# Slot sizes of four SBUF pools rounded to multiples of 256 bytes in a hybrid decoder layer

## The chip, the cores and the metric

The kernel runs on one core of a Trainium2 chip, in one launch. The metric is the device time of the whole program in microseconds (us), as a median of several runs. The profiled execution is one run taken with the hardware profiler; its span reaches from the first to the last instruction.

## The reference

One decoder layer over 2048 tokens of 1024 features, all in float32. Cut to what matters:

```python
h = rmsnorm(x, mix_norm_w)
proj = h @ w_in
y = concatenate([s5_mixer(proj[:, :c_u], ...), ssd_mixer(proj[:, c_u:], ...)])
x = x + y @ w_out                                   # output projection
h = rmsnorm(x, xa_norm_w)
x = x + cross_attention(h, rmsnorm(mem, ...), wq, wk, wv, wo)   # 4 heads, 256 memory tokens
h = rmsnorm(x, ffn_norm_w)
gv = h @ w_up                                       # 1024 -> 2 x 2816
g = causal_dwconv(gv[:, :D_FF], conv_w, conv_b)     # width 3
x = x + (silu(g) * gv[:, D_FF:]) @ w_down           # 2816 -> 1024
return rmsnorm(x, final_norm_w)
```

## The kernel before

**Products.** TensorE multiplies a stationary operand (128 x 128, loaded first) by a moving one (128 x 512). Each float32 operand is split into a high and a low half of 12 significant bits (`halves`, L95: the copy to the high half on ScalarE at L98, the difference to the low half on VectorE at L99). A float32 product is then three matmuls (`mm3`, L123 to L125: high by high, high by low, low by high). So each 512-column float32 product costs one L98, one L99 and a third of the work of the three lines on TensorE. `products` (L999) computes a 2 x 2 block product by seven products instead of eight, in the order `ORDER = (1, 6, 5, 3, 7, 4, 2)`; each of the seven is called m here, and is 12 matmuls long.

**Stages.** They follow one another and share SBUF: when one is over its pools are closed, and the next opens its own over the same bytes.
- Mixer and memory: first norm, input projection, both mixers, keys and values. Not touched. Its pools have names with k, a and s5 in front.
- `stage_b` (L1085): output projection with residual (stationary: halves of y in pool A; moving: W_out in the rings Q0 to Q3), then scores and values of the cross-attention by `products` over eight pairs of token tiles each (stationary: halves of the left factors in A; moving: the right factors in Q0 to Q6). The ring `qp` hands out eight tiles of Q0, then of Q1 and so on, so each m has one Q pool of its own. The first m of each `products`, m = 1, has Q4; m = 6, the second, has Q5; m = 5, the third, Q6; and the last, m = 2, has Q3.
- `stage_up` (L1305): two blocks of 1024 tokens by 22 feature tiles, one `products` each. Stationary: halves of the weights, from the ring `wp`: two tiles at a time from pools V, V, W, W, W, W, W, W, W in turn, a pair (high and low half) for each product, so that of nine products in a row two have V and seven have W. Moving: the right factors in H1 to H7, one pool for each m. Raw weights and factors land in pool R by SyncE's queue (L111) ahead of the split.
- `stage_down` (L1410): seven products m = 0 to 6, each over the eight pairs of token tiles and 11 tiles of features, 33 matmuls for one pair. Stationary: halves of the activations in pools B and C in turn; moving: halves of the weights in the ring W0, W1, W2, W3, W4, eight tiles at a time, 22 tiles for one product. Raw activations land in A, raw weights in R.

**Pools.** `Kit.pools` (L55) lays a stage's pools one behind the other in the order of the call, and all three stages start at the same byte. A slot is as long as the tile (n float32 values per partition), so the lengths are 2048 bytes for n = 512 and 4096 for n = 1024, except for four pools: M in `stage_b` (4 slots of 568 values, of which L1092 uses 512), G and C in `stage_up` (4 slots of 568 values, 520 used; one slot of 992), and O in `stage_down` (2 slots of 1136, 1024 used). `reuse_waits="tile"` makes a new tile wait for the last use of those older tiles that lie on its own bytes. Each engine and each queue takes its instructions in order, so an instruction that waits holds up all that stand behind it on its engine.

Of the kernel before, what the change touches and what calls it, by code (L numbers as in the profile page):

```python
# [9 lines left out]
F32 = mybir.dt.float32  # L10
F32R = mybir.dt.float32r
# [4 lines left out]
P = 128  # L16
# [8 lines left out]
def bcol(a, n):  # L25
    """[p, m] as [p, m, n], each value repeated n times"""
    return a.rearrange("p (a b) -> p a b", b=1).to_broadcast([a.shape[0], a.shape[1], n])


class Kit:  # L30
    """the pools that every stage shares, and the steps that all of them use"""
# [23 lines left out]
    def pools(self, cx, pre, *specs):  # L55
        """pools in this order in memory; each tile waits only for those on its own bytes. A function per pool that takes a tile"""
        def one(nm, bufs, n=512):
            p = cx.enter_context(self.tc.tile_pool(name=pre + nm, bufs=bufs, reuse_waits="tile"))
            return lambda dt=F32: p.tile([P, n], dt, tag=nm, name=nm)
        return [one(*s) for s in specs]  # L60

    def gain(self, i, kt):
        """a norm's weights over feature tile kt, one per partition"""
        return self.gains[:, i * 8 + kt:i * 8 + kt + 1]
# [30 lines left out]
    def halves(self, src, hi, lo, scale=None):  # L95
        """hi + lo = src (times scale), both of 12 significant bits"""
        if scale is None:
            self.S.activation(hi, src, AF.Copy)  # L98
            self.V.tensor_tensor(lo, src, hi.bitcast(F32), op=ALU.subtract)  # L99
        else:  # L100
            self.S.activation(hi, src, AF.Copy, scale=scale)
            self.V.scalar_tensor_tensor(lo, src, scale, hi.bitcast(F32), op0=ALU.mult, op1=ALU.subtract)  # L102
# [24 lines left out]
    def rstd(self, out, ss, scale, eps):  # L127
        """(ss * scale + eps) ** -0.5"""
        n = out.shape[1]
        self.V.tensor_scalar(out, ss, scale, eps, op0=ALU.mult, op1=ALU.add)  # L130
        self.G.tensor_tensor(out, out, self.m05[:, 0:1].to_broadcast([P, n]), op=ALU.pow)  # L131

    def norm(self, x, xs, w=None):
        """xs = x / rms(x) over rows of 1024, times w"""
        ss = self.sm.tile([P, 1], F32, tag="ss", name="ss")
        self.S.activation(xs, x, AF.Square, accum_out=ss)
        self.rstd(ss, ss, 1.0 / 1024, 1e-6)
        if w is None:
            self.V.tensor_scalar(xs, x, ss[:, 0:1], None, op0=ALU.mult)
        else:  # L140
            self.V.scalar_tensor_tensor(xs, x, ss[:, 0:1], w, op0=ALU.mult, op1=ALU.mult)

    def tr4(self, src, hf):
        """four 128-column blocks of src, transposed"""
        p = self.ps()
        for q in range(4):
            c = (hf * 4 + q) * 128
            self.TE.transpose(p[:, q * 128:q * 128 + 128], src[:, c:c + 128], self.ident)
        return p

    def exp(self, pool, x, n, tag):
        """exp to float32's accuracy, for small tiles"""
        V = self.V
# [20 lines left out]
class MixerIn:  # L174
    """first norm, input projection, conv, SSD; blocks of 512 tokens"""

    def __init__(self, k, cx, a, dram, T):
# [40 lines left out]
        self.tri = c([P, P], "tri")                       # 1 where column >= row  # L218
# [8 lines left out]
        self.last = c([P, P], "last")                     # 1 in the last row  # L227
# [12 lines left out]
        self.wd = c([P, 8, 24], "wd", F32R)               # per feature tile, the high parts, then the low ones  # L240
# [24 lines left out]
    def norm1_direct(self):  # L265
        """block 0 straight into its two halves"""
# [51 lines left out]
    def conv(self, p, j):  # L318
        """silu of the causal conv of width 4; the taps are halved, so c * (1 + tanh(c)) is the silu"""
# [14 lines left out]
    def zgate(self, p, i):  # L334
        """2 silu(z)"""
        k = self.k
        th = k.t()
        k.S.activation(th, p, AF.Tanh, scale=0.5)
        z = self.zp.tile([P, 512], F32, tag=f"z{i}", name="z")
        k.V.scalar_tensor_tensor(z, th, 1.0, p, op0=ALU.add, op1=ALU.mult)  # L340
        return z

    def dtprep(self, hs, b):
        k, V, S, TE = self.k, self.k.V, self.k.S, self.k.TE
        p = k.ps()
        for q, (h, l) in enumerate(hs):                    # both parts of the weights with the high ones of h, then high with low
# [14 lines left out]
        s, s2, q = sm("s"), sm("s2"), sm("q")             # log(1 + e) = 2 atanh(e / (2 + e))  # L361
# [38 lines left out]
    def ssd(self, b, pr, dd, xs, Bs, Cs, zs, sqacc):  # L400
        """the six heads of two groups, four chunks of 128 tokens"""
# [3 lines left out]
        L = self.lp.tile([P, 4, 6, P], F32, tag="L", name="L")      # [s, c, h, l] = exp(a_cs[l] - a_cs[s]), 0 for l < s  # L405
# [150 lines left out]
def s5_setup(k, a, d, up, NJ):  # L556
    """the S5 group's step over 8 tokens: input maps, output maps, Toeplitz part, decay and rotations"""
# [22 lines left out]
    # sin and cos, reduced by pi / 2  # L580
# [31 lines left out]
    # powers 0..8 of the transition, [p, g, power]  # L612
# [20 lines left out]
    for s in range(8):                                    # the same, falling  # L633
# [3 lines left out]
    # (transition - 1) / lambda  # L637
# [27 lines left out]
    def comb(gs, A, X, B, Y, op):  # L665
        """[p, 4 g, 8 powers, 16 c] = A * X op B * Y"""
# [95 lines left out]
def stage_s5(k, a, d, T):  # L762
    """S5 group over the whole sequence, as a generator"""
# [132 lines left out]
class Memory:  # L896
    """G = wq k^T and VW = v wo per head, from the normed memory"""
# [4 lines left out]
    def prep(self):  # L902
        k, nc = self.k, self.k.nc
        # features on partitions: [f, (kt pair: kt, m)]
# [15 lines left out]
    def proj(self, name, then, n=1):  # L920
        """(mem w)^T, [d, (d tile pair: d tile, m)]"""
# [21 lines left out]
    def pairs(self, name, at, then):  # L943
        """the split rows of the four heads, one head ahead from piece `at` of the one before"""
# [54 lines left out]
def products(k, terms, tmp, put, after):  # L999
    """The four blocks of a product of 2 x 2 blocks by seven products (Winograd's form), with the left factors  # L1000
    a11, s2 = s1 - a11, s1 = a21 + a22, s4 = a12 - s2, s3 = a11 - a21, a22, a12 (in ORDER) and the right ones
    b11, t2 = b22 - t1, t1 = b12 - b11, b22, t3 = b22 - b12, t4 = t2 - b21, b21.
    put(i, j, x, y, op) takes block (i, j), which is x op y; y (for (1, 0): x) may be written over, but not for (1, 1)"""
# [28 lines left out]
def squares(k, x, junk):  # L1032
    """sum of squares of a row, given as its halves"""
# [14 lines left out]
def h3(k, d, p, x0, x1, tmp):  # L1048
    """right factors of the FFN's first product from the normed rows of a pair of tiles"""
# [29 lines left out]
def ring(n, pools):  # L1079
    """tiles from several pools in turn, n at a time"""  # L1080
# [4 lines left out]
def stage_b(k, cx, a, d, T, after):  # L1085
    """output projection with its residual, cross-attention with its residual, third norm"""
# [5 lines left out]
    xl, xp, q4, mp, ap, *qs, fp = k.pools(cx, "b", ("L", 2, 1024), ("X", 6, 1024), Q(4), ("M", 4, 568), ("A", 16), Q(0), Q(1), Q(2), Q(3), Q(5), Q(6), ("F", 10))  # L1092
# [9 lines left out]
    W, ys = {}, {}  # L1102

    def yprep(t, cuts):
        """halves of y's row of tiles, the columns between cuts at a time"""
# [20 lines left out]
    def factors(nm, j):  # L1126
        """t1, t2, t3, t4 of a right side"""
# [36 lines left out]
    def xprep(p):  # L1164
        xs = []
        for t in (2 * p, 2 * p + 1):
# [4 lines left out]
            k.rstd(rq[t], ss, 256.0 / 1024, 256.0 * 1e-6)      # 1 / (16 rms)  # L1171
# [133 lines left out]
def stage_up(k, cx, a, d, T, NF=22):  # L1305
    """the FFN's two branches, its conv and gate; blocks of 1024 tokens.
    [gate; value] = W^T h by seven products of half-size blocks instead of eight (Winograd's form): over the two branches,
    the two halves of the features and the even and odd tiles of the tokens"""
# [3 lines left out]
    wa, ev, up, h1, gp, wb, cp, *hs, rp, sp = k.pools(cx, "u", ("V", 4), ("E", 8), ("U", 4), H(1), ("G", 4, 568), ("W", 14), ("C", 1, 992), H(3), H(7), H(4), H(2), H(6), H(5),  # L1312
# [15 lines left out]
    def weights(i):  # L1328
        """the seven left factors, one at a time"""
# [27 lines left out]
    def rest():  # L1357
        """third norm of the last pairs of tiles"""
# [51 lines left out]
def stage_down(k, cx, a, d, out, T, NK=11):  # L1410
    """the FFN's output projection with its residual, last norm.
    Seven products instead of eight, one after the other over all pairs of token tiles"""
# [4 lines left out]
    xa, w0, xb, rp, ar, sp, cb, fp, *ws, wr, ca = k.pools(cx, "d", ("X", NT // 2, 1024), W(0), ("Y", NT // 2, 1024), ("O", 2, 1136), ("A", 6), ("S", 2), ("C", 6), ("F", 1, 1024),  # L1417
                                                          W(3), W(4), W(1), W(2), ("R", 4), ("B", 6))
    wp, ac = ring(8, [w0] + ws[2:] + ws[:2]), ring(6, [ca, cb])
    # left: (tile of the pair, half of ff), right: (half of ff, half of d), targets: (tile, half of d, sign)  # L1420
# [125 lines left out]
def layout(inp):  # L1546
    """the inputs as the chip wants them: reshapes, transposes and copies only"""
# [36 lines left out]
```

## Time and profile before

| | us |
|---|---|
| median of 3 runs | 2743.06 (2741.9 to 2744.83) |
| profiled execution, span | 2742.6 |
| ScalarE busy in it | 1322.4 |
| VectorE busy in it | 2119.5 |
| GpSimd busy in it | 484.5 |

The span lies 0.5 us below the median of the runs, and the page tells nothing of what lies around it. In the views, PE is TensorE's matmul, PEld its loading of the stationary operand, DVE is VectorE, ACT ScalarE, POOL GpSimd and SPq SyncE's queue of DMAs. Matmuls overlap one another in the pipe, so a matmul that "takes" 0.39 us can be followed by the next after 0.23 us: the rate is read from start to start. A row of the timeline gives start, duration, engine, line, operation, output and inputs (ps<-H,W: the moving operand lies in one of the H pools and the stationary one in W), count, and in brackets idle time before it with what ended it. Buffer and pool numbers are left out of the names: Q stands for Q0 to Q6, W of `stage_down` for W0 to W4.

### The profile page before, as it was taken

What the parts mean: (1) busy time and instruction counts of PE and PEld (TensorE: products, weight loads), DVE (VectorE), ACT (ScalarE), POOL (GpSimd) and SP (SyncE); (2) the same over time, 40 slices, a digit from 0 to 9 for tenths busy, and PEclk for the clock granted to TensorE, in tenths of its full rate; (3) what the DMA queues carried; (4) which work ended last, traced back from release to release, by engine and by line L of the source; (5) the groups of instructions that cost most, each with busy time, mean ns of one, the idle gap of its engine ahead of it and who ended that gap; (6) DMA issues with size and microseconds to landing.
All of it is one profiled execution on the core that took longest, in us unless ns stands there. A gap on an engine that the chain in (4) does not pass through costs nothing. (4 is left out here: it accounts for less than half of the span.)

```text
span 2742.6 us, 38944 instructions
## 1 busy us (share of the span) xinstructions
PE 2680.1 (98%) x12744; PEld 2201.9 (80%) x12744; DVE 2119.5 (77%) x4032; ACT 1322.4 (48%) x2661; POOL 484.5 (18%) x991
## 2 busy tenths in 40 slices
PE   8999999999899999999999999999999999999997
PEld 6878878787798888887878888888888887788876
DVE  8688887887786646778779778889878777677776
ACT  5565455544445314788635445345434334433333
POOL 0000000159812210201301223111111110000000
PEclk9999999999999999999999999999999999999999
DMA  5453243432377954537753334435222227887886
GB/s 194 139 162 127 90 134 107 122 98 85 110 262 240 334 197 181 183 136 251 249 185 122 119 115 132 126 89 177 86 79 85 77 62 263 276 296 225 261 264 203
DMA packets 238851, 455.57 MB, mean 166 GB/s; under 512 B 29432, under 2 KB 71416, under 8 KB 238648
## 3 DMA queue, kind: packets, MB, share of 16 engines
q1 hardware_dynamic: 182312, 341.38, 37.8%
q0 software_dynamic: 27728, 92.82, 10.5%
q10 hardware_dynamic: 28608, 18.88, 2.2%
q8 instruction: 101, 1.65, 0.3%
q14 instruction: 102, 0.84, 0.1%
HBM read 338.09 MB, written 114.29 MB: 165 GB/s over the span
## 5 line engine op out<-in xcount | busy, mean ns | idle before, releaser
L123 PE MATMUL ps<-H,W 128*128 128x512 f32 x952 | 376.0, 395 | 2.1 <-ACT H L98 2.1
L124 PE MATMUL ps<-H,W 128*128 128x512 f32 x952 | 376.4, 395 | 0.7 <-DVE H L99 0.7
L125 PE MATMUL ps<-H,W 128*128 128x512 f32 x952 | 375.4, 394 | 0.0
L123 PE MATMUL ps<-h,w 128*128 128x512 f32 (+1 forms) x736 | 298.4, 405 | 2.2 <-DVE h L102 1.5
L125 PE MATMUL ps<-h,w 128*128 128x512 f32 (+1 forms) x736 | 285.3, 388 | 0.0
L124 PE MATMUL ps<-h,w 128*128 128x512 f32 (+1 forms) x736 | 284.6, 387 | 0.1
L123 PE MATMUL ps<-Q,A 128*128 128x512 f32 x704 | 276.4, 393 | 1.6 <-ACT M L1010 0.8
L125 PE MATMUL ps<-Q,A 128*128 128x512 f32 x704 | 274.8, 390 | 0.0
L124 PE MATMUL ps<-Q,A 128*128 128x512 f32 x704 | 274.3, 390 | 0.0
L98 ACT ACTIVATE w<-r 128x512 fp32r<-128x512 f32 x224 | 141.2, 635 | 253.9 <-PE ps L124 192.3
L98 ACT ACTIVATE W<-S 128x512 fp32r<-128x512 f32 x191 | 118.8, 629 | 279.5 <-DVE S L1337 140.1
L123 PEld LDWEIGHTS ps<-H,W 128*128 128x128 f32 x952 | 179.3, 188 | 45.4 <-ACT H L98 3.9
L124 PEld LDWEIGHTS ps<-H,W 128*128 128x128 f32 x952 | 179.3, 188 | 44.7 <-DVE H L99 3.2
L125 PEld LDWEIGHTS ps<-H,W 128*128 128x128 f32 x952 | 179.4, 188 | 41.3
L99 DVE TENSOR_TENSOR w<-r,w 128x512 fp32r<-128x512 f32 x224 | 157.3, 704 | 44.3 <-ACT w L98 42.1
L125 PEld LDWEIGHTS ps<-h,w 128*128 128x128 f32 x736 | 138.6, 188 | 29.5
L123 PEld LDWEIGHTS ps<-h,w 128*128 128x128 f32 x736 | 139.0, 189 | 27.7 <-DVE h L102 1.7
L124 PEld LDWEIGHTS ps<-h,w 128*128 128x128 f32 x736 | 139.2, 189 | 25.3 <-DVE h L102 1.1
L123 PEld LDWEIGHTS ps<-Q,A 128*128 128x128 f32 x704 | 132.2, 188 | 29.4 <-ACT M L1010 1.0
L125 PEld LDWEIGHTS ps<-Q,A 128*128 128x128 f32 x704 | 132.1, 188 | 29.1 <-DVE A L99 0.8
L124 PEld LDWEIGHTS ps<-Q,A 128*128 128x128 f32 x704 | 132.2, 188 | 27.3
L98 ACT ACTIVATE A<-F 128x512 fp32r<-128x512 f32 (+1 forms) x146 | 88.9, 630 | 125.6 <-PE ps L124 74.5
(485 smaller groups left out, 6351.9 us busy)
## 6 DMA issues: line engine op xcount, KB each, us to landing
A<-actd SPq DMA_DIRECT2D x192, 256.0 KB, 4.0
r<-in_w_in SPq DMA_DIRECT2D x176, 256.0 KB, 2.9
R<-in_w_up SPq DMA_DIRECT2D x176, 256.0 KB, 2.9
R<-in_w_down SPq DMA_DIRECT2D x132, 256.0 KB, 4.3
actd<-U POOLq DMA_DIRECT2D x88, 256.0 KB, 3.2
A<-actd SPq DMA_DIRECT2D x96, 192.0 KB, 3.7
R<-h3Cd SPq DMA_DIRECT2D x56, 256.0 KB, 3.8
X<-in_x SPq DMA_DIRECT2D x16, 512.0 KB, 6.3
```

The source lines that it names most:

```text
L98: self.S.activation(hi, src, AF.Copy)
L99: self.V.tensor_tensor(lo, src, hi.bitcast(F32), op=ALU.subtract)
L123: self.TE.matmul(out, lh, rh, start=first and i == 0, stop=False)
L124: self.TE.matmul(out, lh, rl, start=False, stop=False)
L125: self.TE.matmul(out, ll, rh, start=False, stop=last and i == n - 1)
```

## The change

M and G get slots of 576 values (2304 bytes), C one of 1024 (4096 bytes), and O slots of 1152 (4608 bytes). No instruction and no tile's used part changes; what changes is where the pools behind these four begin, and with it which older tiles a new tile lies on.

```diff
 def stage_b(k, cx, a, d, T, after):
...
-    xl, xp, q4, mp, ap, *qs, fp = k.pools(cx, "b", ("L", 2, 1024), ("X", 6, 1024), Q(4), ("M", 4, 568), ("A", 16), Q(0), Q(1), Q(2), Q(3), Q(5), Q(6), ("F", 10))
+    xl, xp, q4, mp, ap, *qs, fp = k.pools(cx, "b", ("L", 2, 1024), ("X", 6, 1024), Q(4), ("M", 4, 576), ("A", 16), Q(0), Q(1), Q(2), Q(3), Q(5), Q(6), ("F", 10))
...
 def stage_up(k, cx, a, d, T, NF=22):
...
-    wa, ev, up, h1, gp, wb, cp, *hs, rp, sp = k.pools(cx, "u", ("V", 4), ("E", 8), ("U", 4), H(1), ("G", 4, 568), ("W", 14), ("C", 1, 992), H(3), H(7), H(4), H(2), H(6), H(5),
+    wa, ev, up, h1, gp, wb, cp, *hs, rp, sp = k.pools(cx, "u", ("V", 4), ("E", 8), ("U", 4), H(1), ("G", 4, 576), ("W", 14), ("C", 1, 1024), H(3), H(7), H(4), H(2), H(6), H(5),
                                                       ("R", 8), ("S", 2))
...
 def stage_down(k, cx, a, d, out, T, NK=11):
...
-    xa, w0, xb, rp, ar, sp, cb, fp, *ws, wr, ca = k.pools(cx, "d", ("X", NT // 2, 1024), W(0), ("Y", NT // 2, 1024), ("O", 2, 1136), ("A", 6), ("S", 2), ("C", 6), ("F", 1, 1024),
+    xa, w0, xb, rp, ar, sp, cb, fp, *ws, wr, ca = k.pools(cx, "d", ("X", NT // 2, 1024), W(0), ("Y", NT // 2, 1024), ("O", 2, 1152), ("A", 6), ("S", 2), ("C", 6), ("F", 1, 1024),
                                                           W(3), W(4), W(1), W(2), ("R", 4), ("B", 6))
```

The rest of the diff turns docstrings and comments into blank lines; the line numbers stay.

## The prediction

> **What bounds the kernel now.** I read the page's first part, then the windows by stage, then the groups of instructions by line and shape, then the timeline of TensorE.
>
> ```profile
> span 2742.6 us, 38944 instructions
> ...
> PE 2680.1 (98%) x12744; PEld 2201.9 (80%) x12744; DVE 2119.5 (77%) x4032; ACT 1322.4 (48%) x2661; POOL 484.5 (18%) x991
> ```
>
> TensorE is busy for 98% of the span. The windows split it at the seams of the stages: mixer and memory, `stage_b`, `stage_up`, `stage_down`.
>
> ```profile
> 0.00:897.40 897.40, 864.86 (x4695) 722.73 (x4696) 708.28 (x1709) 471.11 (x994) 221.80 (x537) 0.99 0.45 144
> 897.40:1419.20 521.80, 519.74 (x2443) 432.06 (x2442) 365.56 (x637) 285.80 (x670) 81.25 (x136) 1.00 0.60 210
> 1419.20:2287.75 868.55, 865.08 (x3761) 701.18 (x3760) 715.20 (x1147) 396.16 (x698) 169.64 (x300) 1.00 0.36 113
> 2287.75:2742.60 454.85, 430.43 (x1849) 345.95 (x1847) 330.51 (x544) 169.34 (x303) 11.80 (x19) 0.99 0.80 259
> ```
>
> Columns are the window, its length, then busy time of PE, PEld, DVE, ACT and POOL, granted clock, DMA share, GB/s. `stage_b` and `stage_up` are TensorE alone (520 of 522 and 865 of 869 us, at full clock); in `stage_down` it idles for 24 us. So in these stages what counts is the spacing of matmuls, and a busy row can't show it: PE is busy at any spacing below 0.39 us. The groups show that spacing isn't the same for all.
>
> ```profile
> L124 PE MATMUL ps<-H,W 128*128 128x512 f32 x952 | 376.4, 395 | 0.7 <-DVE H L99 0.7
> L123 PE MATMUL ps<-H,W 128*128 128x512 f32 x952 | 376.0, 395 | 2.1 <-ACT H L98 2.1
> L125 PE MATMUL ps<-H,W 128*128 128x512 f32 x952 | 375.4, 394 | 0.0
> ...
> L125 PE MATMUL ps<-H,V 128*128 128x512 f32 x280 | 109.3, 390 | 0.1
> L124 PE MATMUL ps<-H,V 128*128 128x512 f32 x280 | 109.3, 390 | 0.6 <-DVE H L99 0.5
> L123 PE MATMUL ps<-H,V 128*128 128x512 f32 x280 | 109.1, 390 | 0.0
> ```
>
> The two sorts have the same shape, lines and moving pools, and each product m gets V and W in turn; only the pool of the stationary operand differs. The W sort is 4 to 5 ns dearer. Starts tell it better:
>
> ```profile
> 1600.00 0.40 PE L123 MATMUL ps<-H,W 128*128 128x512 f32 x1
> ...
> 1602.80 0.40 PE L123 MATMUL ps<-H,W 128*128 128x512 f32 x1
> ...
> 2032.73 0.39 PE L123 MATMUL ps<-H,V 128*128 128x512 f32 x1
> ...
> 2035.45 0.39 PE L123 MATMUL ps<-H,V 128*128 128x512 f32 x1
> ...
> 2057.69 0.39 PE L123 MATMUL ps<-H,V 128*128 128x512 f32 x1
> ```
>
> Twelve spacings with W take 2.80 us (233.3 ns each), twelve with V 2.72 (226.7).
>
> **Places.** Count bytes from where the pools of a stage begin, modulo 256. Slots of 2048 and 4096 bytes keep the place. Four slots of 2272 are 9088 = 35 x 256 + 128, one of 3968 is 15 x 256 + 128, two of 4544 are again 9088. So before: in `stage_up` V and H1 lie at 0, W (behind G) at 128, H2 to H7 (behind C too) back at 0. In `stage_b` Q4 is at 0, A and the other Q at 128. In `stage_down` W0 is at 0, and B, C and W1 to W4 at 128. Stationary against moving, the fast V is 0 on 0 and the slow W 128 on 0. If the difference of places is the cause, W0 and Q4 have to be slow and all else at 128 fast. In product m = 3 of `stage_down` the ring gives W0 to feature tiles 7 to 10 and other pools to 0 to 6; in `stage_b` the first product of each pair, m = 1, has Q4.
>
> ```profile
> 2507.63 0.39 PE L123 MATMUL ps<-W,B 128*128 128x512 f32 x1
> ...
> 2510.35 0.39 PE L123 MATMUL ps<-W,B 128*128 128x512 f32 x1
> ...
> 2511.03 0.40 PE L123 MATMUL ps<-W,B 128*128 128x512 f32 x1
> ...
> 2513.82 0.39 PE L123 MATMUL ps<-W,C 128*128 128x512 f32 x1
> ```
>
> ```profile
> 1101.26 0.40 PE L124 MATMUL ps<-Q,A 128*128 128x512 f32 x1
> ...
> 1103.57 0.39 PE L125 MATMUL ps<-Q,A 128*128 128x512 f32 x1
> ...
> 1126.07 0.39 PE L123 MATMUL ps<-Q,A 128*128 128x512 f32 x1
> ...
> 1127.88 0.39 PE L125 MATMUL ps<-Q,A 128*128 128x512 f32 x1
> ```
>
> In `stage_down` twelve spacings take 2.72 us on the other pools (128 on 128) and 2.79 on W0 (128 on 0), with the same line, pool of activations and pair. In `stage_b` ten spacings on Q4 take 2.31 us (231 ns), eight later ones 1.81 (226). Three stages, both roles and both equal places agree: equal is 226.7, unequal 231 to 233.
>
> **The change part by part.** After it 2304 = 9 x 256, 4096 and 4608 = 18 x 256: all operands of the three stages are at 0, which the V rows show at 226.7.
>
> *`stage_up`, spacing.* From 2032.73 to 2057.69 lies one round of the ring: nine products, 108 matmuls, 24.96 us. At 226.7 ns it is 24.48, so a round gives 0.48. There are 44 x 7 = 308 products, 34.2 rounds: **16.4 us**. The means give less (952 x (5 + 5 + 4) ns = 13.3), the single product more (2856 x 6.6 ns = 18.8); the round stands between, so I take it, less 0.2 for its part in the stall below: 16.2. DVE has 715 us of work in 869, so it stays behind TensorE with 16 us less room.
>
> *`stage_b`.* 16 pairs x 12 matmuls x 5 ns (231 against 226) = **1.0 us**, between 0.6 (the transposes ahead of m = 1 may have a share) and 1.2 (at 6.1 ns). The output projection has none: its W_out is in Q0 to Q3.
>
> *`stage_down`.* Eleven tiles for each m, counted along the ring, put W0 under 4, 2, 2, 4, 0, 4 and 0 tiles for m = 0 to 6: 16 tiles x 3 x 8 pairs = 384 matmuls x 5.8 ns = 2.2 us. But there TensorE waits for others:
>
> ```profile
> PE ps L125 <- DVE B L99: 6.5, 8, 1.6
> PE ps L125 <- DVE C L99: 5.4, 4, 2.7
> ```
>
> ```profile
> DVE A L1453 <- DMA A<-actd: 67.7, 62, 3.2
> ```
>
> These waits stand in the products with two activation tiles (m = 0, 1, 5, 6), where DVE waits for loads; time won ahead of such a wait becomes a longer wait. Only m = 2 and 3 surely keep theirs (144 matmuls, 0.8 us). I take **1.3**, between 0.8 and 2.2.
>
> *The seam from `stage_b` to `stage_up`.* Before, R begins at 189184 (the sum of the slots ahead of it: 8192 + 16384 + 8192 + 16384 + 9088 + 28672 + 3968 + 6 x 16384), and F of `stage_b` at 189312. R's first tile thus lies with 128 bytes on the last tile of Q6, which is read by m = 5 of the last pair. After, both begin at 189440. SyncE's queue shows the price:
>
> ```profile
> 1372.36 1.55 SPq L1278 DMA_DIRECT2D X<-x1d  x2
> 1406.47 1.79 SPq L111 DMA_DIRECT2D R<-in_w_up  x4
> ```
>
> ```profile
> SPq L111 <- PE ps L125: 32.4, 1, 32.4
> ```
>
> The first load of `stage_up` waits 32.4 us for a matmul, and all loads stand behind it. What that costs:
>
> ```profile
> 1386.00:1400.00 14.00, 14.00 (x63) 11.60 (x62) 10.98 (x18) 3.50 (x6) 0.25 (x1) 1.00 0.01 1
> 1400.00:1411.20 11.20, 11.20 (x51) 9.20 (x50) 2.77 (x4) 1.23 (x2) 0.81 (x2) 1.00 0.53 189
> 1411.20:1448.00 36.80, 33.42 (x133) 23.43 (x132) 35.22 (x59) 21.51 (x38) 2.66 (x5) 1.00 0.85 285
> ```
>
> DVE idles for 3.0 and 8.4 us, then is busy for 35.2 of 36.8, while TensorE gets through 133 matmuls where 36.8 us at 226.7 ns hold 162. That is 29 x 0.2267 = 6.6 us lost to late halves. Without the overlap R's first tile waits only for F, so the loads come ten and more microseconds earlier, and DVE can do the first splits in its idle 8.4 us. The gain lies between 0 (the four R tiles not held by raw weights may throttle it) and 6.6; the idle time is larger than the loss, so I take **4.5**.
>
> *The other seams.* From `stage_up` to `stage_down` the first tile of A no longer lies on two H3 tiles:
>
> ```profile
> 2279.75 2.72 SPq L111 DMA_DIRECT2D A<-actd  x6
> ```
>
> The group of six can start earlier, but the others in it wait for their own H3 tiles, read by the same product: **0.5**, between 0 and 1.0. Into `stage_b` the change adds overlaps: M's 128 bytes push A, Q and F off the 2048-byte grid of the mixer's pools, so a tile waits for one more. The latest such tile is one of h:
>
> ```profile
> 882.89 0.39 PE L125 MATMUL ps<-t,h 128*128 128x512 f32 x1
> ```
>
> ```profile
> 886.52 0.62 ACT L98 ACTIVATE Q<-F 128x512 fp32r<-128x512 f32 x1
> ```
>
> That matmul ends at 883.3, and ScalarE writes the Q tile that gains the wait at 886.5; the wait is over by 3 us, so nothing queues behind it. Cost 0; if that cover went (ScalarE there 3 us earlier), the later splits on ScalarE and the first matmuls of `stage_b` behind them would wait for what is left of the 3 us.
>
> Sum: 16.2 + 1.0 + 1.3 + 4.5 + 0.5 = 23.5; 2742.6 - 23.5 = 2719.1 for the profiled execution, and with the 0.5 to the median **2719.6 us**.
>
> **The rivals.**
> *The seam gives nothing* (DVE or the R tiles are the limit whenever loads come). For it: DVE's 35.2 of 36.8 busy. Against: the idle time before. 2743.1 - 18.5 = 2724.6.
>
> *Places don't count*, and the change doesn't do what it says: V and W would differ by something else. Only the seams stay: 2743.1 - 5.0 = 2738.1, 0.18% below the median. Against it stand Q4 and W0, slow as moving operands, where W is slow as a stationary one. The Trainium skill, page "TensorE: Matmul & The Clock Gate", section "Wait — 56ns, not 53.3ns?", is on this rival's side: warm spacing there is the columns by the clock plus a fixed bit, 215.7 ns for 512 columns, with no word of places. By it all sorts would be alike; the trace disagrees (226.7 and 233.3). The Trainium skill, page "SBUF — State Buffer", section "A bandwidth-pool intuition that's wrong (but worth ruling out)", gives loads of the stationary operand a second, independent read port, so that its place couldn't matter to the moving one; the W and V rows speak against that too.
>
> *Slower: equal places with the writers.* ScalarE and VectorE now write the halves at the place that TensorE reads. If that cost what unequal operands do, the 840 + 1920 + 1464 = 4224 matmuls that run at 226.7 today would rise by 5.8 ns, 24.5 us, and nothing else be won but the seams: 2743.1 + 24.5 - 5.0 = 2762.6. It decides from the point where engines write at the operands' place; in `stage_b` they do so already (A, Q and F all at 128), at 226 ns in the rows above. So hardly.
>
> **How the numbers follow.** Forecast 0.79; the seam gives nothing 0.13; places don't count 0.05; slower 0.03. A measurement of this kernel can tell about 0.2% (5.5 us) from no change: faster 0.92, within 0.03 + 0.02 = 0.05, slower 0.03. The range takes the forecast's bounds: 2743.1 - (18.8 + 1.2 + 2.2 + 6.6 + 1.0) = 2713.3, and 2743.1 - (13.3 + 0.6 + 0.8) = 2728.4. One more term is uncertain by luck:
>
> ```profile
> 2622.42 0.50 PE L125 MATMUL ps<-W,C 128*128 128x512 f32 x1 [2.73 <-DVE C L99]
> ...
> 2623.95 0.63 PE L124 MATMUL ps<-W,C 128*128 128x512 f32 x1
> 2624.38 0.63 PE L125 MATMUL ps<-W,C 128*128 128x512 f32 x1
> ```
>
> After the longest wait eight matmuls run at 0.43 us, half the clock, about 1.6 us; a shorter wait may lose this, another may gain it. Hence 2712 to 2729, which also covers the first rival.
>
> **What would show it.** The W rows of `stage_up` at 389 to 390 ns like V's, and a round of nine products at 24.48 us; Q4 and W0 stretches at 226.7; R's first load soon after 1373 us, and the stretch to about 1448 us shorter by some 4 us; more idle on TensorE in `stage_down`, not less. Wrong would make it: W rows still at 395 (places), an unchanged stall behind 1419 us (seam), or a new order of instructions at a seam, since the waits by which they are ordered change.

## The result and the profile after

| | before | after |
|---|---|---|
| median | 2743.11 us (2741.9 to 2744.83, 4 runs) | 2718.85 us (2717.87 to 2725.65, 4 runs) |
| profiled execution, span | 2742.6 | 2716.6 |

The ratio is 0.992 (0.9907 to 0.9932): the changed kernel is faster by 24.3 us, 0.9%. The profiled execution of after took 2718.37 us, 1.8 more than its span. If as much lies around the span of before, its profiled execution took 2742.6 + 1.8 = 2744.4, more than the median; so the spans differ by more, 26.0 us.

The first part of the page of after, and the windows between the same seams (columns as above):

```profile
span 2716.6 us, 38961 instructions
...
PE 2656.7 (98%) x12744; PEld 2200.2 (81%) x12744; DVE 2119.4 (78%) x4032; ACT 1322.1 (49%) x2661; POOL 484.6 (18%) x991
```

```profile
0.00:898.09 898.09, 864.96 (x4695) 721.83 (x4695) 710.00 (x1709) 471.95 (x994) 221.96 (x537) 0.99 0.45 144
898.09:1418.47 520.38, 518.27 (x2444) 432.13 (x2442) 371.17 (x646) 290.65 (x678) 81.43 (x136) 1.00 0.62 216
1418.47:2265.14 846.67, 845.47 (x3761) 700.48 (x3760) 708.65 (x1137) 390.72 (x689) 169.35 (x300) 1.00 0.36 114
2265.14:2716.60 451.46, 427.96 (x1849) 345.70 (x1847) 329.55 (x543) 168.81 (x302) 11.85 (x19) 0.99 0.81 260
```

The counts of matmuls are the same, but for one at a seam. `stage_up` lost 21.9 us, `stage_down` 3.4, `stage_b` 1.4, and the mixer is 0.7 longer. The groups of TensorE in `stage_up`:

```profile
L123 PE MATMUL ps<-H,W 128*128 128x512 f32 x952 | 370.7, 389 | 0.0
L125 PE MATMUL ps<-H,W 128*128 128x512 f32 x952 | 370.4, 389 | 0.0
L124 PE MATMUL ps<-H,W 128*128 128x512 f32 x952 | 370.3, 389 | 0.0
...
L123 PE MATMUL ps<-H,V 128*128 128x512 f32 x280 | 109.1, 390 | 0.9 <-ACT V L98 0.9
L125 PE MATMUL ps<-H,V 128*128 128x512 f32 x280 | 109.1, 389 | 0.3 <-DVE V L99 0.3
L124 PE MATMUL ps<-H,V 128*128 128x512 f32 x280 | 108.9, 389 | 0.0
```

The W rows now stand where the V rows stand, and the idle time ahead of them (2.1 and 0.7 us before) is gone. One round of the ring, from the first product with the first V pair to the next of that kind, in TensorE's timeline, and the four W0 tiles of one pair in m = 3 of `stage_down`, to the first matmul of the next pair:

```profile
2014.90 0.39 PE L123 MATMUL ps<-H,V 128*128 128x512 f32 x1
...
2039.38 0.39 PE L123 MATMUL ps<-H,V 128*128 128x512 f32 x1
```

```profile
2502.12 0.39 PE L123 MATMUL ps<-W,B 128*128 128x512 f32 x1
...
2504.84 0.39 PE L123 MATMUL ps<-W,C 128*128 128x512 f32 x1
```

The round takes 24.48 us instead of 24.96, twelve matmuls with W0 2.72 instead of 2.79. At the seam into `stage_up`, first SyncE's queue, then the windows:

```profile
1372.24 1.55 SPq L1278 DMA_DIRECT2D X<-x1d  x2
1373.96 13.65 SPq L111 DMA_DIRECT2D R<-in_w_up  x4
```

```profile
1386.00:1400.00 14.00, 14.00 (x63) 11.58 (x63) 10.75 (x18) 3.49 (x6) 0.53 (x1) 1.00 0.42 132
1400.00:1411.20 11.20, 11.20 (x51) 9.27 (x50) 9.37 (x16) 5.68 (x10) 0.53 (x1) 1.00 0.60 210
1411.20:1448.00 36.80, 36.80 (x164) 30.47 (x163) 35.72 (x61) 23.11 (x39) 3.38 (x6) 1.00 0.75 247
```

The first load of R follows the load ahead of it at once, VectorE works 9.4 us where it worked 2.8, and TensorE gets through 164 matmuls in the 36.8 us instead of 133, without idling. In `stage_down` the waits of TensorE for late halves are as they were:

```profile
PE ps L125 <- DVE C L99: 6.1, 6, 1.6
PE ps L125 <- DVE B L99: 6.0, 7, 2.1
```

To separate two things that a busy row mixes, I took the time from each 512-column matmul's start to the next from the traces. **Spacing** is what the intervals up to 242 ns have above 226.67 each; **stalls** is what the longer ones have above it, the matmuls that start some 0.43 us apart behind a long wait included. In us:

| stage | spacing before, after | stalls before, after | both together |
|---|---|---|---|
| `stage_b` | 2.0, 0.6 | 3.0, 3.0 | -1.4 |
| `stage_up` | 16.45, 0.14 | 7.7, 2.1 | -21.9 |
| `stage_down` | 3.4, 0.85 | 23.0, 22.2 | -3.3 |

So 20.3 us come from the spacing and 6.3 from stalls, 5.6 of them in `stage_up`.

### The profile page after: what moved, and what is told of

Its sections match the earlier page's. It is cut to its first block, busy times and chain, and to the rows that moved or that the text cites. A ratio compares the mean times of both kernels' runs of the same rounds, so it can differ in the third digit from the quotient of the medians.

```text
span 2716.6 us, 38961 instructions
## 1 busy us (share of the span) xinstructions
PE 2656.7 (98%) x12744; PEld 2200.2 (81%) x12744; DVE 2119.4 (78%) x4032; ACT 1322.1 (49%) x2661; POOL 484.6 (18%) x991
## 5 line engine op out<-in xcount | busy, mean ns | idle before, releaser
L123 PE MATMUL ps<-H,W 128*128 128x512 f32 x952 | 370.7, 389 | 0.0
L125 PE MATMUL ps<-H,W 128*128 128x512 f32 x952 | 370.4, 389 | 0.0
L124 PE MATMUL ps<-H,W 128*128 128x512 f32 x952 | 370.3, 389 | 0.0
```

The costliest lines, as they stand in the source:

```text
L123: self.TE.matmul(out, lh, rh, start=first and i == 0, stop=False)
L124: self.TE.matmul(out, lh, rl, start=False, stop=False)
L125: self.TE.matmul(out, ll, rh, start=False, stop=last and i == n - 1)
```

## The experiments

The theory: the spacing depends on the difference of the two operands' places modulo 256 alone, and the stall behind the seam depends on which older tiles lie under the new ones; so the two can be had one without the other. Rivals: the spacing comes from the order of the work, or from absolute places; or the seam gives nothing.

**Seam alone, R.** The kernel before, with 128 bytes between H5 and R, so that R's first tile lies on F only, and a memset of these bytes at the end of `stage_up`. All places of operands stay.

```diff
-    ... H(6), H(5), ("R", 8), ("S", 2))
+    ... H(6), H(5), ("N", 1, 32), ("R", 8), ("S", 2))
...
+    G.memset(pad(), 0.0)
```

> The kernel before, with a pad of 128 bytes ahead of R in stage_up: R's first tile leaves the last tile of Q6, all operands keep their places. Theory (spacing by places, plus the first load's wait): L123 to L125 with W stay at 394 to 395 ns; R's first load is issued near 1374 us instead of 1406; the 6.6 us lost between 1411 and 1448 us shrink by 2 to 6, so 2737 to 2741 us. H6's first tile still lies on the last tile of Q3, which is read to the end of stage_b, so a part may stay. Rival (the seam gives nothing, VectorE is the limit whenever loads come): 2743.

2740.37 us (2737.22 to 2743.32, 11 runs) beside 2741.12 of before (21 runs): 0.9999 (0.999 to 1.0008), nothing. Its loads do start as early as in the changed kernel, 1.7 us behind the start of the same load of X. First its rows of SyncE, then of ScalarE:

```profile
1370.02 1.54 SPq L1278 DMA_DIRECT2D X<-x1d  x2
1371.72 13.62 SPq L111 DMA_DIRECT2D R<-in_w_up  x4
```

```profile
1401.31 2.18 ACT L98 ACTIVATE H<-R 128x512 fp32r<-128x512 f32 x4
1414.25 0.64 ACT L98 ACTIVATE H<-R 128x512 fp32r<-128x512 f32 x1 [10.76 <-PE ps L124]
```

With the data there, the fifth split waits 10.8 us for a matmul. The places say for which: before, counted as in the prediction, H6 begins at 156416 and Q3 ends at 156544, so H6's first tile lies with 128 bytes on the last tile of Q3, which the last product of `stage_b` (m = 2) reads. This second wait stood behind the first and was hidden by it; R's slots then fill up and the queue stops too. Stalls in `stage_up`: 6.6 us, against 7.7.

**Seam alone, R and H6.** The pad is 256 bytes long and stands ahead of H6, so H6, H5 and R leave the last tiles of Q3, Q5 and Q6 and keep their places modulo 256.

```diff
-    ... H(2), H(6), H(5), ("R", 8), ("S", 2))
+    ... H(2), ("N", 1, 64), H(6), H(5), ("R", 8), ("S", 2))
```

> The kernel before, with a pad of 256 bytes ahead of H6 in stage_up: R leaves Q6 and H6's first tile leaves Q3, all operands keep their places modulo 256. Theory: W rows stay at 394 to 395 ns, nearly all of the 6.6 us behind 1411 us goes, 2736 to 2738 us. If the first load alone made the loss, the same as with the pad ahead of R; if H6's wait had a share, 1 to 4 us less than that. Rival (seam gives nothing): 2743.

2737.62 us (2733.67 to 2744.15, 11 runs), 0.9992 (0.9983 to 1.0001): 3.5 us below before's median, at the limit of what can be told. The trace is clearer. The last of the seam's windows in the run with R alone, and in this one:

```profile
1411.20:1448.00 36.80, 33.77 (x137) 24.29 (x136) 33.26 (x55) 21.33 (x38) 3.37 (x6) 1.00 0.67 229
```

```profile
1411.20:1448.00 36.80, 35.95 (x152) 27.81 (x151) 35.10 (x59) 22.18 (x39) 3.52 (x7) 1.00 0.77 258
```

152 matmuls instead of 137, and the stalls of `stage_up` fall from 7.7 us in before to 3.7. In the changed kernel they are 2.1; here R's first load comes at 1387.86 us, not 1373.96: the shift lays R's first tile across two tiles of F, and SyncE waits 14.4 us for a split that reads F.

**Spacing alone.** The changed kernel with M's slots at 592 values, 256 bytes more in all, which brings back the old overlaps at the seam into `stage_up` while all operands stay level. Each engine has its instructions in the order of the kernel before, so a change of order can't be what the spacing comes from here.

```diff
-    ... ("M", 4, 576) ...
+    ... ("M", 4, 592) ...
```

> The kernel after, with M's slots at 592 values: A, Q and F of stage_b move up by 256 bytes, so all operands stay at one place modulo 256, but R's first tile lies on Q6 and H6's on Q3 again, as before. Theory: W rows at 389 ns as after; the first load waits to about 1406 us and 5 to 7 us are lost behind 1411 us; 2724 to 2726 us. Rival (the waits of the seam cost nothing): 2719.

2725.03 us (2720.07 to 2725.44, 5 runs), 0.9942 (0.9929 to 0.9954): 16.1 us below before on its chip. In its groups the W rows are as after, but with the idle time of before:

```profile
L124 PE MATMUL ps<-H,W 128*128 128x512 f32 x952 | 371.2, 390 | 0.7 <-DVE H L99 0.7
L123 PE MATMUL ps<-H,W 128*128 128x512 f32 x952 | 370.9, 390 | 1.4 <-ACT H L98 1.4
L125 PE MATMUL ps<-H,W 128*128 128x512 f32 x952 | 370.5, 389 | 0.0
```

In the trace the spacing is 0.6, 0.4 and 0.8 us in the three stages, and the stalls in `stage_up` are 7.9. With the order of the work unchanged, the spacing goes and the stall stays.

**H moved by 128.** The changed kernel with 128 bytes behind C: H2 to H7 stand 128 off V and W; H1, which lies ahead of C, stays level with both.

```diff
-    ... ("C", 1, 1024) ...
+    ... ("C", 1, 1056) ...
```

> The kernel after, with C's slot at 1056 values: H2 to H7 lie 128 bytes off V, W and H1. Theory (difference of places, whichever operand is ahead): the six products of m = 6, 5, 3, 7, 4 and 2 run at 232 to 233 ns, with V and with W alike, and m = 1 at 226.7; stage_up 3168 x 5.8 ns = 18 us longer, about 2737. Rival (an absolute place of the stationary tile is what is slow): W and V stay at 226.7, 2719. Rival (V against W as such): V fast, W slow.

2750.86 us (one run), 32 us above the changed kernel where 18 were expected. V is now as slow as W:

```profile
L123 PE MATMUL ps<-H,W 128*128 128x512 f32 x952 | 375.7, 395 | 0.1
...
L125 PE MATMUL ps<-H,V 128*128 128x512 f32 x280 | 110.5, 395 | 0.4 <-DVE V L99 0.4
```

By starts both have 233.3 ns over H2 to H7, and over H1 V has 226.7 and W 227.2, in the same stage and between slow neighbours. The spacing is 21.3 us. The other 11 are stalls, 9.9 of them a single one ahead of the first matmul of `stage_down`. That raised a new question: does it belong to the slower matmuls or to the new place of the pools? The next runs take it up.

**W moved by 128 and by 256.** G's slots grow and C's shrinks by as much in all, so that only W (and the small C) move and V, H, R, S stay where the changed kernel has them; every engine has its order of instructions.

```diff
-    ... ("G", 4, 576), ("W", 14), ("C", 1, 1024) ...
+    ... ("G", 4, 584), ("W", 14), ("C", 1, 992) ...
```

> The changed kernel with G's four slots 32 bytes longer and C's slot 128 bytes shorter: in stage_up the ring W lies 128 bytes further on, while V, H1 to H7, R and S and every tile of the other stages lie where they do in the changed kernel. Every engine has its instructions in the changed kernel's order. Theory (what counts is the difference of the two operands' beginnings modulo 256): the H,W rows stand at 394 to 395 ns and 232.4 ns from start to start, the H,V rows stay at 389 and 226.7; 2856 matmuls by 5.7 ns are 16.3 us, no stall at the start of stage_up, and the time is 2718.9 + 16.3 = 2735.2 (2733.5 to 2737). Rival (the gain came only from the order of the work and from which tiles wait): H,W stays at 389, 2717.9 to 2720.

And with G at 592 and C at 960:

> The same with G's slots 64 bytes longer and C's slot 256 bytes shorter: W lies 256 bytes further on, all else as in the changed kernel, order of instructions the same. Theory: a difference of 256 is none, H,W at 389 and 226.7 ns, 2717.9 to 2720.5. Rival (any move of W away from where the change put it costs, by its distance from H or by new waits): 395 and about 2735, or stalls of some us at the start of stage_down.

On one chip, 128 gave 2728.76 us (2728.53 to 2733.18, 5 runs), 0.996 (0.9945 to 0.9976), and 256 gave 2712.56 (2711.47 to 2717.75, 4 runs), 0.9905 (0.9884 to 0.9925). Both lie some 6 us below what was expected, which isn't explained (before was 3.4 us faster on this chip, too), but the difference, 16.2 us, is the 16.3 worked out for it. The groups with 128:

```profile
L123 PE MATMUL ps<-H,W 128*128 128x512 f32 x952 | 376.0, 395 | 0.0
...
L123 PE MATMUL ps<-H,V 128*128 128x512 f32 x280 | 109.0, 389 | 0.0
```

and with 256:

```profile
L123 PE MATMUL ps<-H,W 128*128 128x512 f32 x952 | 370.7, 389 | 0.0
...
L123 PE MATMUL ps<-H,V 128*128 128x512 f32 x280 | 109.0, 389 | 0.0
```

This is the cleanest pair: same instructions in the same order, no stall at the seam (about 1 us of stalls in `stage_up` in both), and 128 bytes under one pool decide over 16 us. Moving W does nothing; moving it by half of 256 does.

**H moved by 256.** As the run with H moved by 128, with its order of instructions, but all operands level.

```diff
-    ... ("C", 1, 1024) ...
+    ... ("C", 1, 1088) ...
```

> The changed kernel with C's slot 256 bytes longer: H2 to H7, R and S lie 256 bytes further on, all operands still begin at the same place modulo 256. Order of the instructions as in the run with H 128 bytes further on. Theory: spacing 226.7 ns for H,W and H,V (389), but the stall of 9.9 us between the last product of stage_up and the first of stage_down comes back, since it belongs to the places of the pools and not to the places modulo 256: 2728 to 2731. Rival (the stall belonged to the slower matmuls, which changed what was late): no stall there, 2718 to 2721.

2730.87 us (2725.44 to 2733.03, 6 runs), 0.9965 (0.9952 to 0.9977). The spacing is 226.7 ns for all, and the stall is there. Rows of TensorE, VectorE and SyncE's queue at the start of `stage_down`:

```profile
2278.13 0.80 PE L123 MATMUL ps<-W,B 128*128 128x512 f32 x1 [9.68 <-ACT B L98]
```

```profile
2270.29 2.73 DVE L1404 SCALAR_TENSOR_TENSOR U<-G,C,U 128x512 f32<-128x512 f32 x4
```

```profile
2273.12 2.73 SPq L111 DMA_DIRECT2D A<-actd  x6
```

The loads of A start 0.1 us after the last L1404 of `stage_up`, which reads C. In the changed kernel A and H3 both begin at 91136 (counted as in the prediction), right behind C; with H3 moved on, C reaches under A's first tile, which then has to wait for C's last reader. The changed kernel loads A nearly nine microseconds before the seam at 2265.14:

```profile
2242.18 14.30 SPq L111 DMA_DIRECT2D R<-in_w_down  x9
2256.53 2.85 SPq L111 DMA_DIRECT2D A<-actd  x6
```

So the stall belongs to the places of the pools, and comes with level operands too. But two waits stand in SyncE's queue here, not one. In the changed kernel H5 ends at 189440, where R of `stage_down` begins; with H5 moved on, its last tile reaches under R's first. In the run with H moved by 256:

```profile
2255.56 15.17 SPq L111 DMA_DIRECT2D R<-in_w_down  x10
```

```profile
SPq L111 <- PE ps L125: 10.2, 1, 10.2
...
SPq L111 <- DVE U L1404: 2.2, 1, 2.2
```

The first load of R waits 10.2 us for a matmul and starts 12.5 us before the last matmul of `stage_up`, against 22.7 in the changed kernel; the loads of A stand behind those of R in the queue, and the wait for C's reader adds 2.2 us and ends last. All five kernels of this study in which C reaches beyond 91136 have a stall of 9.8 to 9.9 us, and none of the others has it; but the same five have H5's last tile under R's first, and an order of instructions of their own on ScalarE, VectorE and SyncE. No run moved A or R alone, so which of these would be enough isn't shown.

**Smaller differences.** Three more runs, one each, all with that stall (9.8 to 9.9 us) in them. Lengths turned out to be rounded up to 32 bytes, so the first of them isn't what its expectation says: W lies 128 bytes further on and H2 to H7 64, which leaves W 64 past H and V 64 short of it.

```diff
-    ... ("G", 4, 576), ("W", 14), ("C", 1, 1024) ...
+    ... ("G", 4, 580), ("W", 14), ("C", 1, 1008) ...
```

> The same with G's slots 16 bytes longer and C's slot 64 bytes shorter: W lies 64 bytes off H modulo 256, V and H as before. At the change from stage_up to stage_down VectorE, ScalarE and the queue of SyncE have their instructions in the order of the run with H 128 bytes further on, which lost 9.9 us there, so the time is the changed kernel's with 10 to 12 us for that, and the spacing on top. Any inequality costs the whole: H,W at 395 and 232.4 ns, 16.3 us. Only half a period costs: 389 and 226.7, nothing. Graded with the distance: half, about 229.5 ns and 8 us. I hold the first, with no row that decides. H,V stays at 226.7 by all three.

With G at 578 and C at 1016:

> G's slots come out 32 bytes longer (a length is rounded up to 32) and C's is 32 bytes shorter, so W lies 128 and H2 to H7 96 bytes further on than in the changed kernel: W stands 32 bytes past H2 to H7, V 96 short of them; against H1 it is W 128, V nothing. The run before of this kind had W 64 past and V 64 short, with 233.2 and 229.6 ns. Any inequality costs: W 230 to 234 ns and V 229 to 234 over the six H. Only from 64 bytes on: W at 226.7 apart from H1's product, which is 0.8 ns on the mean of all. The stall of 9.9 us at the start of stage_down as in the others of this order; 2740 to 2751 or 2731 to 2738.

With G as after and C at 1032:

> C's slot 32 bytes longer: H2 to H7 lie 32 bytes past V and W alike, H1 level with both. Any inequality costs: 229 to 234 ns for W and V over the six H, 226.7 over H1. Only from 64 bytes on: 226.7 everywhere, as with 256. The stall of 9.9 us at the start of stage_down as before; 2740 to 2751 by the first, 2728 to 2732 by the second.

2750.57, 2754.51 and 2749.36 us. The second lies above its range of 2740 to 2751; in it W stands off H1 too, and the spacing of `stage_up` is 23.5 us. All runs together, means from start to start over H2 to H7, inside a product (matmuls 4 to 11 of the twelve), of intervals up to 242 ns:

| stationary less moving, bytes modulo 256 | ns |
|---|---|
| 0 (V or W or both, in eight kernels) | 226.7 to 226.8 |
| 32 (W) | 233.2 |
| 64 (W) | 233.4 |
| 128 (before W, W moved by 128; H moved by 128: W, V) | 232.4, 232.4; 233.3, 233.3 |
| 160 (V) | 233.6 |
| 192 (V) | 228.8 |
| 224 (W, V) | 233.3, 233.3 |

Every difference that was tried costs, and all but one cost 5.7 to 6.9 ns. It is neither graded by the distance nor a matter of half a period. The 192 stands out, in one run and one pool; why is open. With H moved by 32 the group of W over the whole stage reads

```profile
L123 PE MATMUL ps<-H,W 128*128 128x512 f32 x952 | 376.7, 396 | 0.1
```

**Once more, side by side.** The run with W moved by 256 had the lowest median of all; it and the changed kernel were run again on one chip.

> The changed kernel itself, beside the next one on one chip. The run with W 256 bytes further on had the same order of instructions and the same spacing and yet a median of 2712.56 us, 6.3 below the changed kernel's 2718.85, each on a chip of its own. If that is the chip, the two agree within 1.5 us here. If it is the place, this one is the slower by 3 to 6 us, with a stall of about 1 us ahead of the second block of stage_up (V waiting for ScalarE at about 1866 us) and 22 instead of 19.5 us of stalls in stage_down.

> The kernel with W 256 bytes further on once more, beside the changed one on the same chip. By the place: 2712 to 2715, 3 to 6 us below the changed kernel. By the chip: as the changed kernel within 1.5 us.

2719.34 us (2715.44 to 2721.54, 5 runs), 0.9918 (0.9904 to 0.9931), for the changed kernel, and 2716.65 (2713.14 to 2720.28, 4 runs), 0.9911 (0.9898 to 0.9925), for W moved by 256. The first confirms the result; the two can't be told apart, so it isn't shown that the move is worth anything. The medians lie 2.7 us apart, between the two expectations. The traces show one place where they differ: stalls in `stage_down` are 22.2 and 23.0 us in two executions of the changed kernel, and 19.6 and 17.8 in two of the other. Of the former, 1.4 and 2.8 us belong to 7 and 14 matmuls with about 0.43 us from start to start, which the latter don't have. With two of each, chance isn't excluded.

## Why the prediction was right

The forecast was 2719.6 us and the time 2718.85. The mechanism held; that the total came so close is in part luck, for errors of both signs met in it. By steps:

- **`stage_up`, spacing, 16.2 us.** Right: 16.3 from the starts, and 16.2 between the two kernels that differ in nothing else. Of the three ways to size it (group means, one product, one round of the ring) the round was the one that held. The group means gave too little: they are rounded to whole ns, and V's rows stood at 390 in before, a little above the 389 that W reaches after.
- **`stage_b`, 1.0 us.** Right in kind; 1.4 measured. Q4's intervals went from 232.8 ns to 227.2, which is 1.1 us. Another 0.4 us lies in m = 6, which was level already but follows Q4's product: it went from 230.5 to 228.2 ns.
- **`stage_down`, 1.3 us: the step that failed in size.** The spacing gave 2.6. The step cut 2.2 to 1.3 because time won ahead of a wait for VectorE would become a longer wait, and expected more idle time. The waits didn't grow: stalls 23.0 us before, 22.2 after, and TensorE's idle time in the window is 23.5 us after and 24.4 before. From run to run these stalls vary by more than the whole term, so that part can't be shown either way. The term that the prediction left to luck stayed: 8 matmuls of `stage_down` start about 0.43 us apart in before, 7 after.
- **Seam into `stage_up`, 4.5 us.** The size held (5.6 us of stalls gone), the reason only in half. It named R's first tile as the cause, and showed SyncE's wait of 32.4 us for it. Taking that wait away alone gave 1.1 us of stalls and nothing in the median. H6 on Q3 was a second overlap of the same 128 bytes, hidden behind the first, and the change removed both. The prediction read the one wait that the profile showed and didn't go through the places of the other pools.
- **Seam into `stage_down`, 0.5 us.** Not to be told apart: the stalls of the whole stage fell by 0.8 us, less than they vary. That this seam could cost 9.9 us was not seen; the changed sizes happen to bring A and H3 to the same byte, and the end of H5 and R too.
- **Into `stage_b`, nothing.** Right within what two executions can tell; the mixer was 0.7 us longer.
- **Span to median, 0.5 us.** Wrong: it is 1.8. The 0.5 was the difference between one execution and a median of three others. Here luck came in: the span fell by 2.5 us more than forecast (26.0 against 23.5), and 1.3 us more than the 0.5 lie around it; the two errors partly cancel, and the medians differ by 24.3.

The rivals: that places don't count fell with the pair of W moved by 128 and by 256. That the seam gives nothing fell with the run that has the spacing alone: 5.8 us more stalls in `stage_up` than the changed kernel. That equal places cost with the writers fell with the level rows at 226.7 to 226.8 ns in eight kernels, where ScalarE and VectorE write at the same place. The trace goes against the Trainium skill, page "TensorE: Matmul & The Clock Gate", section "Wait — 56ns, not 53.3ns?", as it did before: one warm spacing for 512 columns (215.7 ns there) against 226.7 and 232 to 234 here at a granted clock of 1.00.

## What to carry to other kernels

When two groups of the same matmul differ by some ns in the profile, read start to start and compare where their operands begin: here, bringing the operands of the 512-column products of 32-bit halves to the same place modulo 256 saved 2.5% on those that stood apart, for a few bytes of padding. Why places count at all, no run shows. A pool's length also decides which older tiles the next stage's tiles lie on; lay such a change out for all pools and both seams, since a wait that is removed may have another right behind it, and a shift of 32 bytes put 10 us on a seam here. To price one of the two effects, move a single pool by 128 and by 256 with the rest held in place.

## What was not expected

- A difference of 32 bytes costs as much as one of 128: 233.2 and 233.3 ns against 226.7. Level or not level is what counts.
- With H moved by 128 the intervals don't rise evenly: in long stretches they alternate between 237 and 229 ns, mean 233.3; with W moved by 128 the products average 232.4.
- Where an H1 product (level) follows one that is not level, its first matmuls are slow too, and the later ones fall back to 226.7; with H moved by 32 this takes some seven matmuls. What carries over wasn't tried.
- The mixer's products of h and w are level as well and yet stand at 229.1 ns; no run here touched them.
